# Weights of the feature-major products: high part by a rounding DMA, low part by an accumulating DMA

## The chip, the cores and the metric

The kernel runs on one core of a Trainium2 chip. The metric is the device time of one execution in microseconds (us), lower is better; runs of the kernel before and after are compared as medians. The core has five engines that run apart and meet at semaphores: TensorE (PE, matmul; PEld is its weight load), VectorE (DVE), ScalarE (ACT), GpSimd (POOL) and SyncE (SP, which here only issues transfers). Transfers (DMA) run on 16 DMA engines, whoever issues them.

## What is computed

One encoder layer, in float32, for two requests that share all weights: `p` with 512 positions and `s` with 1024, both 1024 wide.

```python
h = rms_norm(x, g_pre_mix) * (1.0 + sc1) + sh1          # sh, sc, gt: from silu(c) @ w_ada
u = h @ w_in                                            # split into xa, ya, xb, ga, gb
xa = depthwise_conv(xa, conv_w, conv_b, CONV_A_LEFT)
h_fwd, h_bwd = rg_lru(xa, ...), rg_lru(xa, ..., reverse=True)
y_a = ((h_fwd + h_bwd) * jax.nn.gelu(ya)) @ w_a_out
y_b = fourier_mix(xb) @ w_b_out
merged = jax.nn.sigmoid(ga) * y_a + jax.nn.sigmoid(gb) * y_b
x = x + gt1 * rms_norm(merged @ w_o, g_post_mix)
h = rms_norm(x, g_pre_ffn) * (1.0 + sc2) + sh2
up = depthwise_conv(h @ w_up, ffn_conv_w, ffn_conv_b, CONV_F_LEFT)
f = (jax.nn.gelu(gate) * val) @ w_down                  # val, gate: the halves of up
x = x + gt2 * rms_norm(f, g_post_ffn)
```

## The kernel before

**Products.** Every large product runs in three passes on fp32r operands: weight and activation are each split into a high part (the value rounded to fp32r) and a low part (the rest, rounded), and high x high, high x low and low x high are added up in PSUM. In the feature-major products (w_xa, w_ya, w_ga, w_gb, w_a, and w_up for `p` and for three groups of `s`) the weight stands as the stationary operand. `fm_mm` loops over the 8 slices of 128 input rows and in each over the passes in the order of `passes`: weight high with activation high, weight high with activation low, weight low with activation high. So the third matmul of a unit is the first that reads the low part of its weight (in `s`, where each pass has two halves of 512 columns, the fifth).

**Units and steps.** The work is one list of steps. A step may have a `Unit`, a weight tile of 128 x 1024 (512 KB), which is 24 matmuls of 512 columns in `p` and 48 in `s`. In `p` two units fill one PSUM tile, and what follows on ACT and DVE (`post`) comes after the second. `emit` walks the list: before the matmuls of step i it calls `prep_to`, which prepares the units up to three ahead (`AHEAD`), and `load_to`, which issues loads up to three units (`RAW_BUFS`) beyond the prepared ones. The order in which `emit` issues is the order on each engine; nothing is reordered after.

**One unit's weights.** `load_unit` (L124) has SP load the tile into `raw` (3 buffers). `prep_unit` takes an `hl` tile (4 buffers, high and low part) and calls `split`: ACT copies `raw` into the high part (L109; units that are not `on_act` use DVE, L111) and DVE subtracts the high part from `raw` into the low part (L112).

**What stands around them on the queues.** In the first stage of `p`, the recurrent units (`lru_step`) follow each other: after their matmuls ACT runs 8 tanh (L684), 4 exponentials (L692), 4 tanh (L694) and two Relu (L696), later two square roots (L710). The gate products end in a tanh on ACT (L737), the `ya` products in a Gelu on ACT (L776), a product on DVE (L777) and a split (`yh`, `yl`). In the merge stage (`merge_steps`) pairs of w_a units alternate with pairs of w_b units (13 matmuls of 258 columns each), and the RMSNorm of the other request's rows is woven in: ACT squares a row tile with a sum (L413), POOL makes the reciprocal root in two one-column operations (L430, L431), ACT scales (L418). In the up stage of `p` (`up_steps`) 22 pairs of units follow each other; after each pair ACT runs the centre tap (L1339, twice) and DVE the outer taps (L1347), and after every other pair, the gate half, ACT runs the Gelu (L1361). Lines are those of the profile; in the changed file the code below the edits stands 19 lines further down (L696 there is L715, L1361 is L1380).

Of the kernel before, what the change touches and what calls it, by code (L numbers as in the profile page):

```python
# [10 lines left out]
F32 = mybir.dt.float32  # L11
F32R = mybir.dt.float32r
AF = mybir.ActivationFunctionType
ALU = mybir.AluOpType
# [4 lines left out]
KT = D // 128  # L19
# [9 lines left out]

BIG_BUFS = 40  # L30
RAW_BUFS = 3
HL_BUFS = 4
AHEAD = 3
PAIR_AHEAD = 3
# [17 lines left out]
class Seq:  # L52
    def __init__(self, name, idx, n, x, y):
        self.name, self.idx, self.n, self.x, self.y = name, idx, n, x, y
        self.nf = 1024 // n
        self.tt = n // 128
        self.chunks = n // 512
        self.groups = KT // self.nf
        self.pq_tiles = self.tt // 2


class Unit:
    def __init__(self, src, cols, mix=False, on_act=False, whole=True):
        self.src, self.cols, self.mix, self.on_act, self.whole = src, cols, mix, on_act, whole
        self.raw = self.hi = self.lo = None

# [6 lines left out]
class Enc:  # L73
# [46 lines left out]
            nc.vector.tensor_tensor(out=out[:, 1, :], in0=src, in1=out[:, 0, :].bitcast(F32), op=ALU.subtract)  # L120

    def load_unit(self, u):
        u.raw = self.sb.tile([128, u.cols], F32, tag="raw", bufs=RAW_BUFS, name=self.nm("raw"))
        self.nc.sync.dma_start(out=u.raw, in_=u.src)  # L124

    def prep_unit(self, u):
        hl = self.sb.tile([128, 2, u.cols], F32R, tag="hl", bufs=HL_BUFS, name=self.nm("hl"))
        u.hi, u.lo = hl[:, 0, :], hl[:, 1, :]
        src = u.raw
        if u.mix:  # L130
            nc = self.nc
            src = self.big([128, u.cols], name="wb")
            ab = u.raw[:, 0:512].rearrange("p (s c) -> p s c", s=2)
            nc.vector.tensor_tensor(out=src[:, 0:256], in0=ab[:, 0, :], in1=ab[:, 1, :], op=ALU.add)
            nc.vector.tensor_tensor(out=src[:, 256:512], in0=ab[:, 1, :], in1=ab[:, 0, :], op=ALU.subtract)
            nc.vector.tensor_copy(src[:, 512:640], u.raw[:, 512:640])
        if u.mix:
            self.split(u.hi, u.lo[:, 0:512], src, keep=512)
            nc.vector.tensor_tensor(
                out=u.hi[64:96, 512:640], in0=src[64:96, 512:640], in1=u.hi[64:96, 512:640].bitcast(F32), op=ALU.subtract)  # L140
            return
        self.split(u.hi, u.lo, src, act=u.on_act)
# [9 lines left out]

    def load_to(self, k):
        while self.ld < min(len(self.units), k):
            if self.units[self.ld].unit is not None:
                self.load_unit(self.units[self.ld].unit)
            self.ld += 1

    def prep_to(self, k):
        while self.pp < min(len(self.units), k):  # L160
            self.load_to(self.pp + 1)
            u = self.units[self.pp]
            if u.pre is not None:
                u.pre()
            if u.unit is not None and u.unit.whole:
                self.prep_unit(u.unit)
            self.pp += 1
            self.load_to(self.pp + RAW_BUFS)

    def emit(self):  # L170
        pos = 0
        for i, s in enumerate(self.steps):
            while self.rl < min(len(self.steps), i + LOAD_AHEAD + 1):
                for f in self.steps[self.rl].loads:
                    f()
                self.rl += 1
            self.load_to(self.pp + RAW_BUFS)
            self.prep_to(pos + AHEAD + 1)
# [54 lines left out]
    def fm_steps(self, sq, table, tiles, xh, xl, post, on_act=False):  # L233
        box = {}
        steps = []
        for f, m in enumerate(tiles):
            u = Unit(table[m], KT * 128, on_act=on_act)

            def mm(u=u, f=f):
                if f == 0:  # L240
                    box["ps"] = self.ps([128, sq.nf, sq.n])
                self.fm_mm(self.fm_chunks(sq, box["ps"], f), u, 0, xh(), xl())

            steps.append(Step(mm=mm, unit=u))
        steps[-1].post = lambda: post(box.pop("ps"))
        return steps
# [927 lines left out]
    def up_quads(self, sq, hb, dst, plain):  # L1174
# [64 lines left out]
        for g in range(plain, FT):  # L1239
# [3 lines left out]
            def part(i, src, w=w):  # L1243
                if ring["n"] % 2 == 0:
                    ring["t"] = self.sb.tile([128, 2, 1024], F32R, tag="hl", bufs=HL_BUFS, name=self.nm("wq"))
                h = ring["n"] % 2
# [323 lines left out]
```

## Time and profile before

| | us |
|---|---|
| median of 3 runs | 2103.56 |
| their range | 2102.67 to 2103.68 |
| the profiled execution | 2103.23 |
| its span, first to last instruction | 2101.1 |

| engine | busy us | share of the span |
|---|---|---|
| PE | 2068.3 | 98% |
| DVE | 1420.8 | 68% |
| ACT | 944.8 | 45% |
| POOL | 55.3 | 3% |

The profiled execution lies within the range of the timed ones, and 2.1 us of it lie around the span. PE is busy nearly throughout at a granted clock of 0.997, so PE's idle time is the only time that can be taken away without making matmuls fewer or faster; it lies in the first 350 us and at the very end. The trace has about one DMA engine in three busy on the mean (135 GB/s).

### The profile page before, as it was taken

What the parts mean: (1) busy time and instruction counts of PE and PEld (TensorE: products, weight loads), DVE (VectorE), ACT (ScalarE), POOL (GpSimd) and SP (SyncE); (2) the same over time, 40 slices, a digit from 0 to 9 for tenths busy, and PEclk for the clock granted to TensorE, in tenths of its full rate; (3) what the DMA queues carried; (4) which work ended last, traced back from release to release, by engine and by line L of the source; (5) the groups of instructions that cost most, each with busy time, mean ns of one, the idle gap of its engine ahead of it and who ended that gap; (6) DMA issues with size and microseconds to landing.
All of it is one profiled execution on the core that took longest, in us unless ns stands there. A gap on an engine that the chain in (4) does not pass through costs nothing.

```text
span 2101.1 us, 24339 instructions
## 1 busy us (share of the span) xinstructions
PE 2068.3 (98%) x9602; PEld 1687.5 (80%) x9602; DVE 1420.8 (68%) x1798; ACT 944.8 (45%) x1213; POOL 55.3 (3%) x132
## 2 busy tenths in 40 slices
PE   7999999999999999999999999999999999999998
PEld 6777778888888888888888888888888888888887
DVE  4677888677667664656576445749687887875553
ACT  2377555355565632135333336633344444454442
POOL 0000010000000000000100001000000000000000
PEclk9999999999999999999999999999999999999999
DMA  9643475632233314343543324332122222284422
GB/s 342 206 131 130 145 259 188 236 135 96 100 105 99 112 50 145 121 146 122 217 147 116 111 96 166 100 123 88 61 76 83 83 81 81 100 313 165 143 92 109
DMA packets 91121, 284.57 MB, mean 135 GB/s; under 512 B 9056, under 2 KB 20736, under 8 KB 91008
## 3 DMA queue, kind: packets, MB, share of 16 engines
q1 hardware_dynamic: 91008, 283.03, 39.3%
q8 instruction: 75, 1.23, 0.2%
q14 instruction: 38, 0.31, 0.0%
HBM read 237.87 MB, written 45.12 MB: 135 GB/s over the span
## 4 chain that ended last, share of the span: by engine, by line
PE 87%; DVE 5%; ACT 4%; issue 2%; DMA 2%; POOL 0%; SPq 0%; DVEq 0%; POOLq 0%; ACTq 0%
PE ps L201 86%; PE ps L204 1%; DVE hl L112 1%; ACT th L684 1%; ACT th L694 1%; DVE xc L658 1%; ACT ea L692 1%; DMA hr<-hrowp 1%; ACT xn L413 0%; DVE th L715 0%; DVE th L720 0%; DVE th L718 0%; DMA x<-in_x_sample_dram 0%; DMA x<-in_x_prompt_dram 0%; ACT hl L109 0%
## 5 line engine op out<-in xcount | busy, mean ns | idle before, releaser
L201 PE MATMUL ps<-hh,hl 128*128 128x512 f32 x2144 | 632.6, 394 | 3.5 <-DVE hl L112 3.0
L201 PEld LDWEIGHTS ps<-hh,hl 128*128 128x128 f32 x2144 | 402.2, 188 | 99.5 <-DVE hl L112 4.3
L201 PE MATMUL ps<-hl,ah 128*128 128x512 f32 x1440 | 452.3, 395 | 0.0
L112 DVE TENSOR_TENSOR hl<-raw,hl 128x1024 fp32r<-128x1024 f32 (+2 forms) x240 | 286.8, 1200 | 172.3 <-ACT hl L109 170.8
L201 PE MATMUL ps<-hl,hl 128*128 128x512 f32 x1072 | 380.8, 394 | 0.0
L201 PE MATMUL ps<-hx,wq 128*128 128x512 f32 x1596 | 370.9, 394 | 0.0
L109 ACT ACTIVATE hl<-raw 128x1024 fp32r<-128x1024 f32 (+1 forms) x222 | 232.5, 1053 | 279.3 <-PE ps L201 235.2
L201 PEld LDWEIGHTS ps<-hx,wq 128*128 128x128 f32 x1596 | 299.7, 188 | 71.0 <-DVE wq L1251 0.2
L201 PEld LDWEIGHTS ps<-hl,ah 128*128 128x128 f32 x1440 | 269.0, 188 | 61.8
L201 PE MATMUL ps<-hl,al 128*128 128x512 f32 x720 | 283.9, 394 | 0.0
L201 PEld LDWEIGHTS ps<-hl,hl 128*128 128x128 f32 x1072 | 201.4, 188 | 47.6
L201 PEld LDWEIGHTS ps<-hl,al 128*128 128x128 f32 x720 | 135.2, 188 | 32.0
L1347 DVE SCALAR_TENSOR_TENSOR cf<-ps,vec,cf 128x511 f32<-128x511 f32 (+1 forms) x100 | 75.3, 808 | 83.7 <-ACT cf L1339 83.5
L201 PE MATMUL ps<-yh,hl 128*128 128x512 f32 x384 | 111.8, 394 | 0.6 <-DVE yb L991 0.3
L1250 ACT ACTIVATE wq<-wsum 128x512 fp32r<-128x512 f32 x76 | 46.1, 629 | 118.0 <-DVE wsum L1261 118.0
L1195 DVE SCALAR_TENSOR_TENSOR cf<-cq,vec,cf 128x1023 f32<-128x1023 f32 x76 | 97.1, 1277 | 0.0
L1339 ACT ACTIVATE cf<-ps,vec 128x512 f32<-128x512 f32 (+1 forms) x50 | 39.1, 827 | 105.8 <-PE ps L201 105.8
L201 PEld LDWEIGHTS ps<-yh,hl 128*128 128x128 f32 x384 | 71.5, 188 | 17.6 <-DVE yb L991 0.8
L112 DVE TENSOR_TENSOR al<-fq,ah 128x512 fp32r<-128x512 f32 x88 | 57.2, 686 | 32.3 <-PE ps L201 18.4
L201 PE MATMUL ps<-hx,hl 128*128 128x512 f32 x288 | 66.9, 394 | 0.0
L201 PE MATMUL ps<-yl,hl 128*128 128x512 f32 x192 | 65.3, 394 | 0.0
L658 DVE SCALAR_TENSOR_TENSOR xc<-ps,vec,xc 128x511 f32<-128x511 f32 (+3 forms) x48 | 46.9, 1012 | 25.7 <-ACT xc L650 25.1
(182 smaller groups left out, 2325.0 us busy)
## 6 DMA issues: line engine op xcount, KB each, us to landing
raw<-in_w_up_dram SPq DMA_DIRECT2D x88, 512.0 KB, 3.5
raw<-in_w_down_dram SPq DMA_DIRECT2D x66, 512.0 KB, 3.5
ada<-in_w_adaT_dram SPq DMA_DIRECT2D x32, 512.0 KB, 4.9
raw<-in_w_o_dram SPq DMA_DIRECT2D x24, 512.0 KB, 3.5
fs<-cf SPq DMA_DIRECT2D x22, 512.0 KB, 2.6
fq<-fs SPq DMA_DIRECT2D x22, 512.0 KB, 6.0
ada<-in_w_ada_dram SPq DMA_DIRECT2D x16, 512.0 KB, 8.5
raw<-in_w_gb_dram SPq DMA_DIRECT2D x16, 512.0 KB, 4.3
```

Of the source, the lines that this page charges most:

```text
L109: nc.scalar.activation(out=hi, in_=src, func=AF.Copy)
L112: nc.vector.tensor_tensor(out=lo, in0=src[:, 0:keep], in1=hi[:, 0:keep].bitcast(F32), op=ALU.subtract)
L201: self.nc.tensor.matmul(*args, **kw)
L204: self.nc.tensor.transpose(*args)
L658: nc.vector.scalar_tensor_tensor(out=xc[:, f, o], in0=ps[:, f, o.start + d:o.stop + d], scalar=w[:, tap:tap + 1], in1=xc[:, f, o], op0=ALU ...
L684: nc.scalar.activation(out=t[:, f, :], in_=ps[:, f, :], func=AF.Tanh, scale=0.5, bias=self.halfb[:, b:b + 1])
L692: nc.scalar.activation(out=ea[:, f, :], in_=r[:, f, :], func=AF.Exp, scale=self.nk4[:, k:k + 1], bias=self.nk4[:, k:k + 1])
L694: nc.scalar.activation(out=r[:, f, :], in_=r[:, f, :], func=AF.Tanh, scale=self.k2[:, k:k + 1], bias=self.k2[:, k:k + 1])
L1195: nc.vector.scalar_tensor_tensor(out=box[key][:, o], in0=c[:, i], scalar=self.vec[:, V_FW + 3 * m + t:V_FW + 3 * m + t + 1], in1=box[key][ ...
L1250: nc.scalar.activation(out=hi, in_=src, func=AF.Copy)
L1339: nc.scalar.activation(out=acc[:, f, :], in_=ps[:, f, :], func=AF.Identity, scale=w[:, 1:2], bias=self.vec[:, V_FB + m:V_FB + m + 1])
L1347: nc.vector.scalar_tensor_tensor(out=acc[:, f, o], in0=ps[:, f, o.start + d:o.stop + d], scalar=w[:, tap:tap + 1], in1=acc[:, f, o], op0=A ...
```

## The change

The units of the feature-major products (118 in all: 34 in the mixing and merge stages of `p`, 32 in the heads and `ya` of `s` and 8 in its merge, 44 in the up stage of `p`) no longer use `raw` or DVE. Their `hl` tile is taken at the load. POOL issues a DMA that reads the weight and writes it rounded to fp32r into the high part (L128 of the changed file); ACT writes the negated high part into the low part (L135, the same size as the copy that it replaces); then POOL issues a second DMA that reads the weight again and adds it onto the low part (L136). `load_to` holds such a unit back until it is at most one beyond the next to be prepared, and `prep_to` prepares it one step later than other units, after it has issued the next unit's load.

```diff
+DMA_LO = True
     def load_unit(self, u):
+        if u.dma:
+            hl = self.sb.tile([128, 2, u.cols], F32R, tag="hl", bufs=HL_BUFS, name=self.nm("hl"))
+            u.hi, u.lo = hl[:, 0, :], hl[:, 1, :]
+            self.nc.gpsimd.dma_start(out=u.hi, in_=u.src)
+            return
...
     def prep_unit(self, u):
+        if u.dma:
+            self.nc.scalar.activation(out=u.lo, in_=u.hi.bitcast(F32), func=AF.Copy, scale=-1.0)
+            self.nc.gpsimd.dma_start(out=u.lo, in_=u.src, accum_op=ALU.add)
+            return
...
     def load_to(self, k):
         while self.ld < min(len(self.units), k):
+            u = self.units[self.ld].unit
+            if u is not None and u.dma and self.ld > self.pp + 1:
+                return
...
     def prep_to(self, k):
         while self.pp < min(len(self.units), k):
             self.load_to(self.pp + 1)
             u = self.units[self.pp]
+            if u.unit is not None and u.unit.dma and self.pp + 2 > k:
+                break
+            if u.unit is not None and u.unit.dma:
+                self.load_to(self.pp + 2)
...
-            u = Unit(table[m], KT * 128, on_act=on_act)
+            u = Unit(table[m], KT * 128, on_act=on_act, dma=DMA_LO)
```

ACT in the first recurrent step of `p`, kernel before: the end of the recurrent unit's chain (the names `th`), and the copy `hl_1214`, which belongs to the fourth unit that PE runs after the recurrent one.

```order
L694 ACTIVATE th_1179<-th_1179,k_104 128x512
L696 ACTIVATE th_1179<-th_1179 128x1024
L109 ACTIVATE hl_1214<-raw_1075 128x1024
L710 ACT_TABLE_LOAD
L710 ACTIVATE th_1159<-th_1159 128x1024
L710 ACTIVATE th_1179<-th_1179 128x1024
L650 ACTIVATE xc_1282<-ps_1219,vec 128x512 x2
```

The same place of the changed kernel; `hl_1098` belongs to the third unit after the recurrent one, `hl_1143` to the fourth.

```order
L713 ACTIVATE th_1168<-th_1168,k_104 128x512
L715 ACTIVATE th_1168<-th_1168 128x1024
L135 ACTIVATE hl_1098<-hl_1098 128x1024
L729 ACT_TABLE_LOAD
L729 ACTIVATE th_1148<-th_1148 128x1024
L729 ACTIVATE th_1168<-th_1168 128x1024
L135 ACTIVATE hl_1143<-hl_1143 128x1024
```

The third unit's ACT instruction moved from a place ahead of the whole chain to the place behind its last Relu, and the fourth's from there to behind the square roots. The other three recurrent steps of `p` show the same.

ACT in the up stage of `p`, kernel before: centre taps and Gelu of one pair (`cf_8434`, from `ps_8377`), then the copies for the fourth and the fifth unit that PE runs after that pair.

```order
L1339 ACTIVATE cf_8434<-ps_8377,vec 128x512 x2
L1361 ACTIVATE cf_8434<-cf_8434 128x1024
L109 ACTIVATE hl_8442<-raw_8333 128x1024
L109 ACTIVATE hl_8474<-raw_8373 128x1024
L1339 ACTIVATE cf_8504<-ps_8449,vec 128x512 x2
```

The changed kernel, a Gelu of the same kind; `hl_8415` and `hl_8446` belong to the third and the fourth unit after the pair `ps_8419`.

```order
L1358 ACTIVATE cf_8473<-ps_8419,vec 128x512 x2
L1380 ACTIVATE cf_8473<-cf_8473 128x1024
L135 ACTIVATE hl_8415<-hl_8415 128x1024
L135 ACTIVATE hl_8446<-hl_8446 128x1024
L1358 ACTIVATE cf_8542<-ps_8489,vec 128x512 x2
```

Each copy stands one unit later on ACT against PE's work than it did.

POOL in the merge stage of `p`, kernel before: only the two operations of each RMSNorm.

```order
L430 TENSOR_SCALAR sm_2384<-sm_2380 128x1
L431 TENSOR_TENSOR sm_2381<-sm_2384,mhalf 128x1
L430 TENSOR_SCALAR sm_2414<-sm_2410 128x1
L431 TENSOR_TENSOR sm_2411<-sm_2414,mhalf 128x1
L430 TENSOR_SCALAR sm_2449<-sm_2445 128x1
L431 TENSOR_TENSOR sm_2446<-sm_2449,mhalf 128x1
```

The changed kernel at the first w_a pair behind w_b units (`hl_2291`, `hl_2340`): DMA rows stand among them.

```order
L128 DMA hl_2340<-in_w_a_dram 128x1024
L449 TENSOR_SCALAR sm_2356<-sm_2352 128x1
L450 TENSOR_TENSOR sm_2353<-sm_2356,mhalf 128x1
L449 TENSOR_SCALAR sm_2381<-sm_2377 128x1
L450 TENSOR_TENSOR sm_2378<-sm_2381,mhalf 128x1
L136 DMA hl_2291<-in_w_a_dram 128x1024
L449 TENSOR_SCALAR sm_2415<-sm_2411 128x1
L450 TENSOR_TENSOR sm_2412<-sm_2415,mhalf 128x1
L136 DMA hl_2340<-in_w_a_dram 128x1024
```

The RMSNorm operations now queue behind the loads of high parts, each of which waits for PE to be done with the unit that held its buffer.

## Rows read from the trace of the kernel before

**Rows 1.** The page, busy us (share of the span) and instructions by engine.
```profile
PE 2068.3 (98%) x9602; PEld 1687.5 (80%) x9602; DVE 1420.8 (68%) x1798; ACT 944.8 (45%) x1213; POOL 55.3 (3%) x132
```

**Rows 2.** Busy time by stretch: from:to, length, busy us of each engine, PEclk, DMA share, GB/s.
```profile
100.00:150.00 50.00, 43.67 (x218) 34.84 (x217) 36.73 (x41) 32.96 (x42) 0.00 (x0) 1.00 0.40 129
150.00:200.00 50.00, 48.82 (x212) 39.25 (x211) 37.25 (x36) 39.48 (x49) 0.00 (x0) 1.00 0.47 158
200.00:250.00 50.00, 47.15 (x201) 37.20 (x200) 40.17 (x41) 34.38 (x40) 0.00 (x0) 1.00 0.36 127
250.00:300.00 50.00, 46.75 (x231) 38.52 (x230) 45.63 (x79) 21.35 (x30) 5.81 (x8) 0.97 0.67 230
...
1100.00:1200.00 100.00, 100.00 (x433) 80.84 (x432) 61.90 (x81) 35.17 (x41) 0.00 (x0) 1.00 0.33 111
```

**Rows 3.** Waits of PE over the span: waited for, us in total, times, longest.
```profile
PE ps L201 <- DVE hl L112: 4.9, 8, 1.9
```

**Rows 4.** The page's costliest groups: busy us, mean ns of one | idle before, releaser.
```profile
L112 DVE TENSOR_TENSOR hl<-raw,hl 128x1024 fp32r<-128x1024 f32 (+2 forms) x240 | 286.8, 1200 | 172.3 <-ACT hl L109 170.8
```

**Rows 5.** DMA issues: out<-in, queue, count, size, median us from issue to landing.
```profile
raw<-in_w_up_dram SPq DMA_DIRECT2D x88, 512.0 KB, 3.5
...
ada<-in_w_ada_dram SPq DMA_DIRECT2D x16, 512.0 KB, 8.5
```

**Rows 6.** Timeline, first recurrent step of p: start us, us, engine, line, operation.
```profile
116.47 4.72 ACT L684 ACTIVATE th<-ps,halfb 128x512 f32<-128x512 f32 x8
...
128.53 1.06 ACT L696 ACTIVATE th<-th 128x1024 f32<-128x1024 f32 x1
129.50 1.04 ACT L109 ACTIVATE hl<-raw 128x1024 fp32r<-128x1024 f32 x1
129.95 0.63 PE L201 MATMUL ps<-hh,hl 128*128 128x512 f32 x2
```

**Rows 7.** Timeline, the same two rows in the third and the fourth recurrent step.
```profile
200.29 1.04 ACT L109 ACTIVATE hl<-raw 128x1024 fp32r<-128x1024 f32 x1
...
202.05 0.63 PE L201 MATMUL ps<-hh,hl 128*128 128x512 f32 x2
...
231.51 0.62 PE L201 MATMUL ps<-hh,hl 128*128 128x512 f32 x2
231.55 1.04 ACT L109 ACTIVATE hl<-raw 128x1024 fp32r<-128x1024 f32 x1
```

**Rows 8.** Timeline, up stage of p: the copies behind one Gelu, and a later matmul.
```profile
1120.99 1.99 ACT L109 ACTIVATE hl<-raw 128x1024 fp32r<-128x1024 f32 x2
...
1127.12 0.63 PE L201 MATMUL ps<-hh,hl 128*128 128x512 f32 x2
```

**Rows 9.** Timeline, merge stage of p: last Gelu of ya and PE's matmuls.
```profile
266.88 1.03 ACT L776 ACTIVATE gl<-ps 128x1024 f32<-128x1024 f32 x1 [1.95 <-PE ps L201]
...
271.82 0.39 PE L201 MATMUL ps<-yh,hl 128*128 128x512 f32 x1
...
285.20 0.65 PE L201 MATMUL ps<-z,hl 128*128 128x258 f32 x4
...
295.65 0.62 PE L201 MATMUL ps<-yh,hl 128*128 128x512 f32 x2
...
306.34 0.52 PE L201 MATMUL ps<-z,hl 128*128 128x258 f32 x3
...
309.93 0.39 PE L201 MATMUL ps<-yh,hl 128*128 128x512 f32 x1
```

**Rows 10.** Timeline, merge stage of p: the RMSNorm on POOL and ACT.
```profile
311.36 0.51 POOL L430 TENSOR_SCALAR sm<-sm 128x1 f32<-128x1 f32 x1 [5.33 <-ACT xn L413]
311.95 0.55 POOL L431 TENSOR_TENSOR sm<-sm,mhalf 128x1 f32<-128x1 f32 x1
312.53 1.15 ACT L418 ACTIVATE xn<-x,sm 128x1024 f32<-128x1024 f32 x1 [1.26 <-POOL sm L431]
...
314.54 1.05 ACT L413 ACTIVATE xn<-x 128x1024 f32<-128x1024 f32 x1
```

More of the change, by code (lines that the diff above doesn't have):

```diff
@@ L62, with __init__ @@
 class Unit:
-    def __init__(self, src, cols, mix=False, on_act=False, whole=True):
+    def __init__(self, src, cols, mix=False, on_act=False, whole=True, dma=False):
+        self.dma = dma
         self.src, self.cols, self.mix, self.on_act, self.whole = src, cols, mix, on_act, whole
```

## The prediction

> **What bounds the kernel now.** First the page's engine line: PE is busy for 2068.3 of 2101.1 us [rows 1]. A stretch in which PE never idles holds 433 matmuls in 100 us, 0.231 us each [rows 2], so a unit is 24 x 0.231 = 5.56 us of PE in `p` and 11.1 us in `s`. Only idle time of PE can be won, and the busy times by stretch say where it is: 6.33 + 1.18 + 2.85 + 3.25 = 13.6 us between 100 and 300 us, the four stretches in which PE falls short of 50 [rows 2], and none in the up stage of `p`. Then the waits of PE: the largest part that has a name in those stretches is the DVE subtract, 4.9 us in 8 waits [rows 3]. So DVE work matters in the first 300 us and nowhere else, though 118 of the 240 subtracts (1200 ns each, 142 us) go [rows 4].
>
> **What the change removes.** 118 subtracts on DVE: 84 of them (40 in `s`, 44 in the up stage) lie beside a PE that never waits for them and are worth nothing. The 34 in the first stages of `p` take 34 x 1.2 = 41 us of load off DVE where it holds PE up. I credit all the idle time of 100 to 300 us, less the 3.25 us of the last stretch, which stay in the reckoning of the merge stage below: **-10.4 us**. The removed loads on SP (3.5 us to landing [rows 5]) were hidden three units ahead: nothing. ACT's negated copy is of the size of the one it replaces: nothing by itself.
>
> **What it adds: a landing behind ACT's copy.** Before, 1.2 us of DVE lay between ACT's copy and a usable low part. Now a transfer lies there, L us from the copy's end to landing. No row shows an accumulating DMA, nor one that POOL issues. Below: 3.5 us, the same 512 KB read once by SP [rows 5]. Above: 8.5 us, the slowest group of 512 KB, when all DMA engines are busy [rows 5]. I take L = 6, nearer to the middle than to either row: 3.5, plus 1.1 for a turn of POOL (its nearest row, the pair of one-column operations from 311.36 to 312.50 [rows 10]), plus 1.5 for reading as many bytes again: at a DMA share of 0.33 the trace moves 111 GB/s, 336 at full share [rows 2], and 524 KB at 336 GB/s take 1.56 us. The Trainium skill ("DMA: Bandwidth & Descriptors", Anatomy of one DMA) fits a transfer issued by GpSimd as 2.0 us plus bytes at 436 GB/s, an estimate of 3.2 us here and about that of our lower row; the total by it would be 2120.
>
> **What it moves.** The order rows show that ACT's copy stands one unit later against PE's work than before. Where that puts it behind a chain that starts at PE's last pair, a lead that was comfortable is used up. The low part is needed by a unit's third matmul.
>
> *Heads of `p`, four recurrent steps.* The third unit behind the recurrent one is now copied where the fourth was: behind the last Relu. That place ends at 129.50 + 1.04 = 130.54, and the third unit's third matmul started at 129.95 [rows 6]: 0.6 us too late before the transfer has begun. ACT's chain there is its own (tanh from 116.47 on [rows 6]), so less DVE work doesn't shorten it. In the third step the place ends 0.7 us before the matmul, in the fourth 1.1 us behind it [rows 7]; the second is like the first. Mean 0.4 too late: 4 x (L + 0.4) = **+25.6 us**. The fourth unit's low part comes behind the square roots, some 4 us later, and PE reaches it 5.56 us later: covered.
>
> *Up stage of `p`, 22 pairs.* Behind the Gelu of every second pair stand two copies, 1120.99 to 1122.98, the first done at about 1122.0 [rows 8]. In the changed order it serves the unit whose third matmul ran at 1127.12 [rows 8]: lead 5.1 us. The second has 5.56 - 0.95 us more and is covered, as are the copies behind the pairs without a Gelu. 11 x (L - 5.1) = **+9.9 us**. The high part is loaded once PE has left a buffer, three units or 16.7 us ahead, and its landing plus the copy fit into that: nothing.
>
> *Merge stage of `p`, four pairs of w_a units.* First pair: the copy is now behind the last `ya` split, a chain that starts with the Gelu at 266.88: 1.03, the product on DVE and the split's copy 1.2 + 1.05, this copy 1.05, done at 271.2; the third matmul was at 271.82 [rows 9]. L - 0.6 = +5.4. Third pair: POOL's RMSNorm operations now queue behind a high part's load, which waits for PE to finish the second w_a unit before it; ACT's scaling waits for POOL, and the copy stands behind two such rounds on ACT. From PE's last matmul of that unit (just before 306.5 [rows 9]): one issue on POOL, at a price of 1, then 1.1, scaling 1.15, squares 1.05 + 0.2, 1.1, 1.15 [rows 10], copy 1.05: 7.8 us, plus L. PE's third matmul of the third pair starts at 309.93 [rows 9], only 3.4 us after the same point. L + 4.4 = +10.4. Second pair: the same 7.8 + L from 285.85 (end of the w_b unit's matmuls that start at 285.20), against 295.65 [rows 9], 9.8 us with the stalls of before in them: +4.0. Fourth pair: no RMSNorm stands ahead, only one POOL issue: 1 + L - 3.6 = +3.4. Together **+23.2 us**.
>
> *Queues passed.* On POOL only the RMSNorm operations are overtaken; in the row stages their results wait for no one on PE. SP loses 118 loads and its other loads come no later. In `s` a unit lasts 11.1 us, so a copy one unit later still leaves one whole unit, 11 us, for L: nothing.
>
> **Sum.** -10.4 + 25.6 + 9.9 + 23.2 = +48 us on the profiled 2103.2 (span 2101.1 and 2.1 around it; the median is 0.3 above): **2151.5**. At L = 3.5: heads 15.6, up 0, merge 2.9 + 1.5 + 7.9 + 0.9 = 13.2, sum +18, so 2122. At L = 8.5: 35.6, 37.4, 33.2, sum +96, so 2199.
>
> **Rivals.**
>
> *The transfers do not keep up* (slower still). In the up stage a unit's plain load is 0.524 MB in 5.56 us, 94 GB/s or a share of 0.28; the rest of the 0.33 [rows 2] is 0.05. If the rounding and the accumulating DMA take c plain loads of DMA time together, the share is 0.05 + 0.28 c, over 1 from c = 3.4. At c = 5 (rounding twice a plain load, adding three times) it is 1.45: 44 x 5.56 x 0.45 = 110 us, and between 100 and 300 us, where the mean share is 0.475, of which 34 x 1.56 / 200 = 0.265 are the 34 loads, 0.21 + 5 x 0.265 = 1.53: 200 x 0.53 = 106 us. With little of the short leads beside it, about 2320; from c = 4 on it is over 2200. For it: nothing bounds c from above in this trace. Against it: only the second read is certain, c = 3, a share of 0.89. The Trainium skill ("Collectives: The Full Stack", The bandwidth ceiling) says that an add inside the DMA costs two source reads and no cycles of its own; no run here shows it, and by it the add alone would not saturate.
>
> *Faster.* DVE's relief counts in full and the low parts land in time, at 2103.2 - 10.4 = 2093. It is decided in the recurrent steps and the merge stage: the sum of the terms above passes zero at L of about 0.8 us, under any landing in the trace. So it needs the copies to run earlier than ACT's order and chain say, by five us or so at each of the four recurrent steps; DVE's relief could do that only if it shortened ACT's chain, which waits for PE and itself.
>
> *No change* needs the same with a part of the landing left: 2099 to 2107.
>
> **How the numbers follow.** About 0.2%, 4 us, is what a measurement of this kernel can tell from no change. Short leads with L between 3.5 and 8.5, taken 10 us wider below since DVE's relief may also pull some copies forward, and 15 wider above for longer landings when DMA is crowded: 2112 to 2215, chance 0.74. Transfers that do not keep up: 0.16, 2200 to 2340. Faster 0.06, no change 0.04. The range reaches from 2112 to 2260: it leaves out 0.10 below and about 0.10 of the saturated cases above. Faster 0.06, same 0.04, slower 0.90; the predicted time is that of the likeliest case.
>
> **What would show each step.** 122 subtracts left on L112 and 118 fewer rows on DVE. PE waiting for a DMA onto `hl` four times between 110 and 260 us by some 6 us each, four times in the merge stage by 3 to 10, and at every fourth unit of the up stage by about 1; no such wait in `s`. The median time from issue to landing of the accumulating DMA gives L, and with it each term. PE's waits for DVE in the first 300 us gone. A DMA share near 1 and waits at every unit of the up stage would show the first rival; a landing behind the copy that PE doesn't wait for in the recurrent steps would show that the order was read wrongly.

## The result, and the profile after

The changed kernel takes 2185.09 us (median of 4 runs, 2184.3 to 2185.7) against 2103.37 us before: a ratio of 1.0389, 95% interval 1.0371 to 1.0407. It is 81.7 us slower; 48 were forecast, and the time lies inside the range of 2112 to 2260 that was given. The profiled execution spans 2182.9 us against 2101.1, which is 81.8 more.

The page of the changed kernel: busy time by engine; the DMA queues (packets, MB, share of 16 engines; SP's loads are q1, POOL's are q0); the subtracts that are left; the landing times.

```profile
PE 2092.9 (96%) x9602; PEld 1702.7 (78%) x9602; DVE 1287.4 (59%) x1680; ACT 946.2 (43%) x1213; POOL 223.0 (10%) x368
...
q1 hardware_dynamic: 74016, 221.16, 28.7%
q0 software_dynamic: 33984, 123.75, 25.2%
...
L114 DVE TENSOR_TENSOR hl<-raw,hl 128x1024 fp32r<-128x1024 f32 (+3 forms) x122 | 144.0, 1180 | 108.6 <-ACT hl L111 107.7
...
hl<-in_w_up_dram POOLq DMA_DIRECT2D x88, 512.0 KB, 6.9
...
raw<-in_w_up_dram SPq DMA_DIRECT2D x44, 512.0 KB, 3.4
```

Two readings answer to [rows 1]. PE's idle time went from 2101.1 - 2068.3 = 32.8 us to 2182.9 - 2092.9 = 90.0 us, 57.2 more. And PE's *busy* time grew by 24.6 us with the same 9602 matmuls. Together they are the 81.8 us, and the second part stands nowhere in the prediction's sum. DVE lost 133 us of work, as meant, and POOL gained 168 us of issuing.

The waits of PE over the span, to be set beside [rows 3]: what was waited for, us in total, times, longest.

```profile
PE ps L220 <- DMA hl<-in_w_a_dram: 27.8, 5, 10.7
PE ps L220 <- DMA hl<-in_w_up_dram: 16.1, 12, 5.3
PE ps L220 <- DMA hl<-in_w_gb_dram: 13.1, 3, 5.5
...
PE ps L220 <- DMA hl<-in_w_ya_dram: 6.7, 2, 5.2
PE ps L220 <- DMA hl<-in_w_xa_dram: 4.9, 1, 4.9
...
PE ps L220 <- DVE hl L114: 0.4, 2, 0.2
```

The waits for the split weights are 27.8 + 16.1 + 13.1 + 6.7 + 4.9 = 68.6 us in 23 places. The idle time that is left, 90.0 - 68.6 = 21.4, is 11.4 less than before. Most of that is DVE's relief: the wait for the subtract fell from 4.9 to 0.4. Some of it may be that PE, held up at the new waits, finds other work done.

Where the 24.6 us of busy time come from is seen in the stretches (from:to, length, PE busy, granted clock, DMA share, GB/s):

```profile
100.00:150.00 50.00, 45.06 (x241) 0.93 0.65 163
...
300.00:350.00 50.00, 37.77 (x175) 0.80 0.75 229
350.00:400.00 50.00, 37.07 (x161) 0.80 0.55 155
```

Before, PE's clock was 1.00 in nearly all of this part [rows 2]. Closer, around one wait of the merge stage (the same columns, 2 us each), and the start of PE's rows behind that wait (start, duration, engine, line, operation):

```profile
328.00:330.00 2.00, 0.00 (x0) 0.50 0.92 176
...
336.00:338.00 2.00, 2.00 (x9) 0.83 0.08 27
338.00:340.00 2.00, 2.00 (x10) 1.00 0.00 0
```

```profile
331.17 1.22 PE L220 MATMUL ps<-yh,hl 128*128 128x512 f32 x2 [5.99 <-DMA hl<-in_w_a_dram]
332.19 0.63 PE L220 MATMUL ps<-yl,hl 128*128 128x512 f32 x1
332.62 1.05 PE L220 MATMUL ps<-yh,hl 128*128 128x512 f32 x2
```

In this wait the granted clock is 0.50, the lower of its two levels (1.2 of 2.4 GHz); it had fallen between 322 and 324 us, at two shorter waits of PE. When the low part lands, matmuls start 0.43 us apart (332.19, 332.62) instead of 0.23, for some 5 us; then the clock is back. PE's rows show the same behind each of the eight long waits of `p`'s first stages, behind the long one of the up stage, and behind two shorter ones (2.7 and 1.9 us): six to thirteen matmuls 0.43 us apart, 1.3 to 2.5 us lost at each. Taken together, PE is busy for 55.4 us at 0.50 in the changed kernel and for 6.8 before. At full clock the same work takes half of that, so 24.3 of the 24.6 us are the clock.

Before, no wait between 30 and 350 us was longer than 1.9 us, but one of that length was followed by such a stretch, in the merge stage (PE's rows before; twelve matmuls of 258 columns take 1.62 us ahead of the wait and six take 1.49 behind it):

```profile
283.37 1.62 PE L201 MATMUL ps<-z,hl 128*128 128x258 f32 x12
...
289.76 0.98 PE L201 MATMUL ps<-z,hl 128*128 128x258 f32 x6 [1.86 <-DVE mg L1000]
...
293.06 1.49 PE L201 MATMUL ps<-z,hl 128*128 128x258 f32 x6
```

The granted clock is 0.50 from 291.2 to 294.6 us there, which is the 0.97 of the stretch from 250 to 300 in [rows 2]. The same holds at the start of that trace, from 28.3 to 31.8 us, where matmuls of 512 columns start 0.43 us apart. Behind the other wait of 1.86 us before, which ends at 244.61, nothing is slow. So a wait of just under 2 us can go either way, and each of the changed kernel's nine longest waits for a low part (3.96 to 10.73 us) is followed by a slow stretch.

The Trainium skill has this ("TensorE: Matmul & The Clock Gate", HAM oscillation): a wait for a DMA between tiles sends PE back to half clock, and the cost is paid at every such wait. The trace agrees for those nine waits, and the prediction had left it out.

### The profile page after: what moved, and what is told of

It is laid out like the page before. It is cut to its first block, busy times and chain, and to the rows that moved or that the text cites. A ratio compares the mean times of both kernels' runs of the same rounds, so it can differ in the third digit from the quotient of the medians.

```text
span 2182.9 us, 24512 instructions
## 1 busy us (share of the span) xinstructions
PE 2092.9 (96%) x9602; PEld 1702.7 (78%) x9602; DVE 1287.4 (59%) x1680; ACT 946.2 (43%) x1213; POOL 223.0 (10%) x368
## 3 DMA queue, kind: packets, MB, share of 16 engines
q1 hardware_dynamic: 74016, 221.16, 28.7%
q0 software_dynamic: 33984, 123.75, 25.2%
## 4 chain that ended last, share of the span: by engine, by line
PE 83%; DMA 7%; issue 6%; ACT 2%; POOL 1%; DVE 0%; SPq 0%; POOLq 0%; DVEq 0%; ACTq 0%
PE ps L220 82%; DMA hl<-in_w_up_dram 3%; DMA hl<-in_w_a_dram 1%; PE ps L223 1%; DMA hl<-in_w_ya_dram 1%; DMA hl<-in_w_gb_dram 1%; POOL hl L128 0%; ACT th L713 0%; DMA wxbt<-in_wxbT_dram 0%; ACT hl L135 0%; ACT ea L711 0%; DMA hl<-in_w_xa_dram 0%; ACT xn L432 0%; POOL sm L450 0%; POOL sm L1112 0%
## 5 line engine op out<-in xcount | busy, mean ns | idle before, releaser
L220 PE MATMUL ps<-hh,hl 128*128 128x512 f32 x2144 | 645.5, 401 | 40.9 <-DMA hl<-in_w_up_dram 16.1
L220 PEld LDWEIGHTS ps<-hh,hl 128*128 128x128 f32 x2144 | 408.2, 191 | 145.5 <-DMA hl<-in_w_up_dram 21.4
L220 PE MATMUL ps<-hl,hl 128*128 128x512 f32 x1072 | 386.0, 399 | 0.0
L114 DVE TENSOR_TENSOR hl<-raw,hl 128x1024 fp32r<-128x1024 f32 (+3 forms) x122 | 144.0, 1180 | 108.6 <-ACT hl L111 107.7
L135 ACT ACTIVATE hl<-hl 128x1024 fp32r<-128x1024 f32 x118 | 123.1, 1051 | 135.6 <-DMA hl<-in_w_up_dram 70.7
L111 ACT ACTIVATE hl<-raw 128x1024 fp32r<-128x1024 f32 (+1 forms) x104 | 109.7, 1055 | 166.3 <-PE ps L220 144.8
L220 PE MATMUL ps<-yh,hl 128*128 128x512 f32 x384 | 119.3, 415 | 28.9 <-DMA hl<-in_w_a_dram 27.8
L220 PEld LDWEIGHTS ps<-yh,hl 128*128 128x128 f32 x384 | 75.9, 200 | 48.5 <-DMA hl<-in_w_a_dram 30.2
L1101 POOL TENSOR_SCALAR sm<-sm 128x1 f32<-128x1 f32 x48 | 10.8, 229 | 820.4 <-ACT junk L1099 819.6
L114 DVE TENSOR_TENSOR al<-fq,ah 128x512 fp32r<-128x512 f32 x88 | 57.3, 687 | 32.9 <-PE ps L220 18.4
L722 DVE SCALAR_TENSOR_TENSOR th<-th,xc 128x1024 f32<-128x1024 f32 x24 | 29.3, 1225 | 71.0 <-ACT th L703 69.5
```

What stands on the lines that cost most here:

```text
L111: nc.scalar.activation(out=hi, in_=src, func=AF.Copy)
L114: nc.vector.tensor_tensor(out=lo, in0=src[:, 0:keep], in1=hi[:, 0:keep].bitcast(F32), op=ALU.subtract)
L135: self.nc.scalar.activation(out=u.lo, in_=u.hi.bitcast(F32), func=AF.Copy, scale=-1.0)
L220: self.nc.tensor.matmul(*args, **kw)
L722: nc.vector.scalar_tensor_tensor(out=i, in0=i, scalar=1.0, in1=xc, op0=ALU.add, op1=ALU.mult)
L1101: nc.gpsimd.tensor_scalar(out=sums[o][:, half:half + 1], in0=sums[o][:, half:half + 1], scalar1=1.0 / D, scalar2=sums[o][:, 0:1] if half e ...
```

## The waits, seen one by one

First recurrent step of `p`, changed kernel (timeline, columns as above; in brackets the idle time before and what ended it): the copy of the third unit, its accumulating DMA, and PE's third matmul of that unit.

```profile
129.09 1.04 ACT L135 ACTIVATE hl<-hl 128x1024 fp32r<-128x1024 f32 x1
...
130.57 0.87 POOL L136 DMA_DIRECT2D hl<-in_w_gb_dram  x1 [10.12 <-ACT hl L135]
...
136.01 1.22 PE L220 MATMUL ps<-hh,hl 128*128 128x512 f32 x2 [4.94 <-DMA hl<-in_w_gb_dram]
```

The copy ends at 130.13 and PE starts at 136.01: L = 5.9 us, where 6 was taken. The copy ends 0.9 us before PE first needs the low part (136.01 - 4.94 = 131.07), where the prediction had it 0.6 us behind in this step, so the wait is 4.94 and not 6.6.

Third pair of the merge stage: POOL's load of a high part behind PE, the RMSNorm on POOL and ACT, the copy, the DMA, PE.

```profile
345.03 0.61 POOL L128 DMA_DIRECT2D hl<-in_w_a_dram  x1 [12.56 <-PE ps L220]
...
347.59 1.15 ACT L437 ACTIVATE xn<-x,sm 128x1024 f32<-128x1024 f32 x1 [12.90 <-POOL sm L450]
...
351.77 1.04 ACT L135 ACTIVATE hl<-hl 128x1024 fp32r<-128x1024 f32 x1
...
358.98 1.22 PE L220 MATMUL ps<-yh,hl 128*128 128x512 f32 x2 [10.73 <-DMA hl<-in_w_a_dram]
```

The RMSNorm of another request's rows stands still on POOL behind a load that waits for PE, ACT waits 12.9 us for it, and the copy behind it ends at 352.81: 7.8 us behind the load's issue, the 7.8 of the prediction. From there to PE's matmul are 6.2, and PE waits 10.7 (10.4 were forecast).

Up stage, the longest wait:

```profile
1236.30 0.87 POOL L136 DMA_DIRECT2D hl<-in_w_up_dram  x1 [5.87 <-ACT hl L135]
...
1236.87 0.86 POOL L128 DMA_DIRECT2D hl<-in_w_up_dram  x1
...
1237.44 1.19 POOL L136 DMA_DIRECT2D hl<-in_w_up_dram  x1
...
1246.51 1.22 PE L220 MATMUL ps<-hh,hl 128*128 128x512 f32 x2 [5.26 <-DMA hl<-in_w_up_dram]
```

Three weight transfers are issued within 1.2 us on POOL (and five loads on SP from 1235.96 to 1238.06), and the first of them lands 10.2 us after its issue; at most of the other Gelus the first low part lands after 5.1 to 6.4. The other eleven waits of this stage are 16.1 - 5.3 = 10.8 us. Eight of them stand at units whose copy is the first behind a Gelu, as forecast, and come to 6.9 us. Three, 3.9 us, stand at other units at the start of the stage (PE's matmuls at 1110.11, 1131.00 and 1138.30), where low parts landed 7.8 to 13 us after their issue and the DMA share was 0.97 (1110 to 1160 us); no term had these.

## The experiments

The theory at the start: a low part that is copied one unit later and then lands 5.9 us after the copy comes too late at the places that the prediction names, and each long wait costs a stretch at half clock besides. The rivals: the rate of the DMA engines; the position alone, whatever makes the low part; the adding DMA as such; stages that act on each other. Where a run is compared with the kernel before, that is the one that ran on the same chip beside it (2103.1 to 2104.5 us); a comparison with the changed kernel is across chips, and good to 1 or 2 us.

**Filling the waits (e1).** PE repeats a harmless first matmul while it would wait.

```diff
+WARM = {6: 20, 10: 20, 16: 22, 20: 21, 26: 21, 28: 24, 30: 44, 32: 16}
...
+        if u.dma:
+            for _ in range(WARM.get(self.seen, 0)):
+                for out, cols in outs:
+                    self.mmul(out, lhsT=u.hi[:, 0:128], rhs=xh[0][:, cols], start=True, stop=True)
+            self.seen += 1
```

> The changed kernel with one thing added: ahead of eight units (the four units of the recurrent steps and the four w_a units at which PE waited 4 to 11 us for a low part) PE runs the unit's first matmul 16 to 44 times more, so that it is busy for most of the wait and nothing starts earlier. Theory (a long wait costs twice: the wait, and then 9 to 13 matmuls at a granted clock of 0.5, 0.43 us each instead of 0.23): the waits stay as long but are filled, the eight slow stretches go, 8 x 2.3 = 18 us less, 2167 us. Rival (the slow matmuls come from the transfers that run beside them, or from the unit's place in the program): they stay, 2185 us or a little above. Second rival (filling the wait makes it longer): above 2186.

Measured: 2171.9 us, 13.2 less than the changed kernel, by doing 188 matmuls more. The page's engine line and the same stretches as above:

```profile
PE 2120.0 (98%) x9790; PEld 1725.8 (80%) x9790; DVE 1287.2 (59%) x1680; ACT 945.9 (44%) x1213; POOL 222.4 (10%) x368
```

```profile
100.00:150.00 50.00, 49.72 (x274) 1.00 0.70 173
...
300.00:350.00 50.00, 46.63 (x230) 0.97 0.81 267
350.00:400.00 50.00, 49.28 (x241) 1.00 0.54 148
```

The granted clock is 1.00 where it was 0.93 and 0.80, at about the same DMA share or a higher one, so the transfers are not what slowed the matmuls. 188 x 0.231 = 43.4 us of PE's busy time are the repeats; the rest is 2120.0 - 43.4 = 2076.6, 16.3 us less than in the changed kernel. Only 13.2 of them reach the time, since idle time and repeats together are 50.0 + 43.4 = 93.4 us against 90.0 idle before: the waits became 3.4 us longer in all. The 18 us of the expectation were a little high because a slow stretch costs nearer 2.0 us than 2.3. Five waits of 2 to 5 us stay unfilled, and behind three of them the clock still falls. The clock part of the loss is shown.

**The low part last (e2).**

```diff
-        for k in range(nk):
-            for q, (w, x) in enumerate(self.passes(u, xh, xl)):
+        for k, q in sorted(((k, q) for k in range(nk) for q in range(3)), key=lambda t: u.dma and t[1] == 2):
+            w, x = self.passes(u, xh, xl)[q]
```

> The changed kernel with the three passes of a feature-major unit in another order: the sixteen matmuls that read the high part first, then the eight that read the low part, so the low part is needed at the seventeenth matmul instead of the third, 14 x 0.231 = 3.2 us later in p. Theory (short leads before the low part): every wait shrinks by 3.2 us. Recurrent steps and ya 23 to 7 us of waits, merge 26 to 13, up 16 to 2, and the slow stretches go wherever the wait falls under 2 us, which leaves one or two of ten (22 of 24.5 us go): 2185 - 43 - 22 = 2120 us. Rival (the DMA engines do not keep up, so that the waits are a matter of rate): a later need delays nothing in the long run, the waits come back at later units, above 2165 us.

Measured: 2136.2 us (2134.4 and 2138.0), 49 us less than the changed kernel with the same transfers; 65 were expected. The waits for `w_up` fall from 16.1 to 4.5 us, those for `w_a` from 27.8 to 13.7. A rate limit would not yield to this, so lead time is the matter. Of the shortfall some 9 us are waits for low parts, 31.1 us where 22 were expected, most of them in the recurrent steps and `ya` (12.9 for 7) and in the up stage (4.5 for 2). Some 7 us are slow stretches: PE's busy time fell by 15.3 us and not by 22. The merge stage came out as expected in sum, but not evenly:

```profile
PE ps L220 <- DMA hl<-in_w_a_dram: 13.7, 4, 9.7
```

The longest wait there, at the third pair, is still 9.7 us. A PE that comes sooner to it finds the same chain of POOL and ACT, which is argued from the rows and not tested.

**The order alone (e3).** The kernel before, its splits issued one unit later.

```diff
             u = self.units[self.pp]
+            if u.unit is not None and u.unit.late and self.pp + 2 > k:
+                break
...
-            u = Unit(table[m], KT * 128, on_act=on_act)
+            u = Unit(table[m], KT * 128, on_act=on_act, late=True)
```

> The kernel before with only the move: feature-major units are prepared one unit later, as in the change, but still loaded by SP and split by ACT and DVE. Theory (the late copy costs because a landing of 5.9 us stands behind it): with 1.2 us of DVE in its place the four recurrent steps cost 4 x (0.4 + 1.4) = 7 us, the up stage nothing since its lead is 5 us, the merge stage 1 or 2, and no wait is long enough to bring the clock down: 2110 to 2114 us. Rival (the position alone is the cost, through ACT's and DVE's queues): above 2130. No change at all would say that leads are not used up by the position.

Measured: 2133.9 us, 29 us slower than the kernel before (ratio 1.0141, 1.0112 to 1.0171). The theory, at 7 to 10 us, fell here, and so did its word that no wait would bring the clock down: PE's idle time grew by 18.1 us and its busy time by 11.9 (2080.2 of 2131.1 us). A wait of PE, and what stands ahead of it on ACT and DVE:

```profile
PE ps L204 <- DVE hl L113: 26.8, 14, 4.9
```

```profile
132.08 1.04 ACT L110 ACTIVATE hl<-raw 128x1024 fp32r<-128x1024 f32 x1
...
138.38 1.23 DVE L726 TENSOR_TENSOR th<-th,th 128x1024 f32<-128x1024 f32 x1
139.52 1.22 DVE L113 TENSOR_TENSOR hl<-raw,hl 128x1024 fp32r<-128x1024 f32 x1
...
140.80 1.22 PE L204 MATMUL ps<-hh,hl 128*128 128x512 f32 x2 [4.80 <-DVE hl L113]
```

It is another unit that waits: the fourth, whose copy now stands behind the square roots. The copy is done at 133.1, but the subtract queues on DVE behind the scans and products of the recurrent step until 139.52. In the changed kernel the same copy is followed by a DMA, which does not queue on DVE, and PE doesn't wait there. So the late position is costly with either means of making the low part, but by different waits: with DVE at the fourth unit, through DVE's queue; with the DMA at the third, through the landing. The 29 us are not a part of the 82 that could be taken off them.

**A plain second DMA (e4).**

```diff
-            self.nc.gpsimd.dma_start(out=u.lo, in_=u.src, accum_op=ALU.add)
+            self.nc.gpsimd.dma_start(out=u.lo, in_=u.src)
```

> The changed kernel with the second DMA as a plain rounding write instead of an accumulating one, so the low part holds the rounded weight (the product is another, the work and the order are the same). Theory (the landing of 5.9 us is that of a transfer issued by POOL, rounding or adding alike: in the trace the rounding ones take 6.2 us from issue to landing and the accumulating ones 6.4): landing 6 to 6.4 us, time 2175 to 2186. Rival (adding is what costs): landing near the 3.5 us of SP's plain loads, waits of 2.4 us less at each site, most slow stretches gone, about 2125 us.

Measured: 2149.4 us in the one run, 36 less than the changed kernel. Neither side of the expectation held: the landing falls, but not to SP's.

```profile
PE 2084.0 (97%) x9602; PEld 1699.5 (79%) x9602; DVE 1287.1 (60%) x1680; ACT 944.3 (44%) x1213; POOL 179.6 (8%) x368
...
q0 software_dynamic: 33984, 123.75, 18.4%
...
hl<-in_w_up_dram POOLq DMA_DIRECT2D x88, 512.0 KB, 4.5
```

The 236 rounding loads use 18.4% of 2147.6 us on the 16 DMA engines, 1.67 us each. With 118 of them accumulating it was 25.2% of 2182.9, 550 us; less 118 x 1.67 that is 353, or 2.99 us for an accumulating one, if the rounding ones beside it still take 1.67. SP's queue uses 28.7% of 2182.9 us for 221.16 MB of all its transfers, on the mean 1.48 us for 0.524 MB. So an accumulating transfer costs 2.0 plain ones of DMA time, and both together c = 3.1. The Trainium skill ("Collectives: The Full Stack", The bandwidth ceiling) counts two source reads and no extra cycles for an add. The 2.0 fits it; that the second read is what takes the time, no run shows.

The landing follows: the median is 4.5 us for a load issued by POOL when nothing adds, and 6.2 (rounding) and 6.4 (accumulating) when half of them add. Whether the others land later because they share POOL's queue or because they share the 16 DMA engines is not told apart. Of L some 1.9 us are the add; 1.0 is POOL's issue against SP's. Of the 35.3 us by which the span is shorter, 26.4 are idle time of PE (63.6 against 90.0) and 8.9 are busy time. The forecast's terms give nearly that idle time for 1.9 us of landing, 4 x 1.9 + 11 x 0.9 + 4 x 1.9 = 25.1, and have nothing for the busy time.

**One stage at a time (e5, e6, e12).** In each run only the named units carry the change.

```diff
-            u = Unit(table[m], KT * 128, on_act=on_act, dma=DMA_LO)
+            u = Unit(table[m], KT * 128, on_act=on_act, dma=DMA_LO and table is self.a["w_up"] and sq.name == "p")
```

> The change in the up stage of p alone (44 of the 118 units); the rest as before. Theory (the cost is the sum of local waits and the slow clock behind the long ones): what that stage gave in the changed kernel, 16 us of waits and 7 us of slow matmuls, 2103 + 23 = 2126 us, and PE's waits at every second pair. Forecast of the step as written: 10 us, 2113. Rival (the stages act on each other, by the queue of POOL or by the buffers): off by over 5 us from 2126.

> The change in the units of s alone (40 of 118); the rest as before. Theory: a unit lasts 11.1 us there, so one later leaves room for a landing; only one wait of 2.0 us stood there in the changed kernel: 2103 to 2106 us. Rival (twice the weight traffic and POOL's queue cost everywhere): 2110 or above. Rival on the other side (less DVE work helps in s): 2101 or below.

> The change in the first stages of p alone (34 of 118: recurrent heads, ya, merge). Theory (the stages add up): the whole change is 81.7 us, the up stage alone gave 21.4 and s alone 3.6, so 56.7 are left: 2160 us, 2157 to 2163. Rival (the stages act on each other, so that the parts do not add up): off by over 5 us from it.

Measured against the kernel before beside each: the up stage 2124.5 us, +21.4; `s` 2106.7, +3.6 (ratio 1.0015, 1.0004 to 1.0025); the first stages of `p` 2157.0, +53.8. The sum is 78.8 of 81.7 us, so the parts add up to within 3. That is a little luckier than it looks: in the trace of the up stage's run, stretches at half clock stand also at 110 to 114 and 247 to 250 us, behind waits of 1.6 and 1.9 us in parts that this run doesn't change, and cost some 3 of the 21.4 us. The up stage has 11.4 us of waits for `hl` here instead of 16.1, with a longest of 3.7 instead of 5.3; why is not shown. In `s` 1.8 us are one wait for `w_a`; less DVE work helps nothing there.

**The most that can be won (e7).**

```diff
+        if u.nosub:
+            self.nc.scalar.activation(out=u.hi, in_=src, func=AF.Copy)
+            u.lo = u.hi
+            return
```

> The kernel before without the subtract of the feature-major units on DVE: the third pass reads the high part again (so the product lacks its low x high part), and nothing takes the subtract's place. It prices what the change can give at most. Theory: the waits of PE for DVE between 100 and 300 us, 13.6 us of idle time, of which I credited 10.4: 2092 to 2096 us. Rival (DVE's other work or ACT's chain ends last there anyway): 2099 or above.

Measured: 2089.3 us, ratio 0.9936 (0.9921 to 0.9951): 13.9 us faster, with PE busy for 2063.9 of 2087.1 us. Idle time fell by 9.6 us and busy time by 4.4; the slow stretch at 291 us is gone with them. That prices the subtract's removal with nothing in its place; this kernel leaves out the product of the low weight with the high activation. With the other steps as they stand, a change that takes the subtract away can win 14 us, and this one put 68.6 us of waits there.

**The copy a unit earlier (e8, e9, e10).** A fifth buffer lets the copy stand where it stood before the change. In e8 the next high part is issued behind this unit's low part (`more` is 0 throughout), in e9, whose edit stands here, ahead of it; e10 is e9 with the low part last. Room for the buffer comes from three small tags.

```diff
-HL_BUFS = 4
+HL_BUFS = 5
...
-            if u is not None and u.dma and self.ld > self.pp + 1:
+            if u is not None and u.dma and self.ld > self.pp + more:
...
-            if u.unit is not None and u.unit.dma and self.pp + 2 > k:
-                break
             if u.unit is not None and u.unit.dma:
-                self.load_to(self.pp + 2)
+                self.load_to(self.pp + 2, 1)
```

> The changed kernel with a fifth buffer for the split weights (room made in three small tags), so that ACT's copy stands one unit earlier, where it stood before the change; all else as in the change. Theory (the lead that was used up is one unit, 5.6 us in p): waits in the recurrent steps fall from 5 us to 0 or 1, those of the merge stage by 5 us each (about 6 us are left, most at the third pair), the up stage has none, one slow stretch is left: 2095 to 2106 us. Rival (rate of the DMA engines, share 0.83 in the up stage): above 2140. Rival (POOL's queue: a high part's load that waits for PE holds up the low part's transfer behind it whatever the order): above 2120.

Measured: 2346.6 us, far on the other side. The up stage of e8, ACT and POOL:

```profile
1200.80 0.86 POOL L136 DMA_DIRECT2D hl<-in_w_up_dram  x1 [12.82 <-ACT hl L135]
1201.36 0.88 POOL L128 DMA_DIRECT2D hl<-in_w_up_dram  x1
...
1207.84 1.06 ACT L135 ACTIVATE hl<-hl 128x1024 fp32r<-128x1024 f32 x1 [6.13 <-DMA hl<-in_w_up_dram]
...
1209.33 0.86 POOL L136 DMA_DIRECT2D hl<-in_w_up_dram  x1 [7.10 <-ACT hl L135]
```

From one low part's issue to the next are 8.5 us: the high part's issue, its landing, the copy. PE needs a new unit every 5.56 us, so this chain sets the pace. It was the edit's order on POOL that made it, not the earlier copy, as e9 shows.

> As e8_early (five buffers, ACT's copy one unit earlier, where it stood before the change), but the next unit's high part is issued on POOL ahead of this unit's low part, as in the change. In e8_early it stood behind it, and the units became a chain: low part issued, next high part issued, some 6 us of landing, copy 1.05 us, next low part issued, 8.4 us a unit where PE needs 5.56. Theory (position): the waits of 5 us in the recurrent steps and ya go, in the merge stage 5 us of the third pair and one slow stretch (2.4) are left, the up stage waits under 5 us in all, and DVE's relief is what the kernel without the subtract gained, 14 us: 2103 - 14 + 5 + 2 + 3 = 2099, range 2092 to 2108. Rival (the transfers' rate, or ACT's queue standing still for the high part, 6.2 us of landing against 5.56 us of PE a unit): waits in the up stage at most units, above 2120.

> e9_five and the pass order of e2_lo_last together: the copy a unit earlier, and the low part needed 3.2 us later. Theory: what waits are left in e9_five shrink by 3.2 us each; at most one of 2 us stays (third pair of the merge stage): 2089 to 2096 us, faster than the kernel before by 7 to 14 us. Rival (waits of ACT for high parts set the pace): as far above as e9_five, less a few us.

Measured: e9 2130.4 us, e10 2123.1 us, ratios 1.0127 (1.0110 to 1.0144) and 1.0092 (1.0077 to 1.0107). The earlier copy, with the fifth buffer that it needs, takes back 55 of the 82 us, so most of the loss is the position. But 2092 to 2108 had been expected of e9 and 2089 to 2096 of e10. What is left in e9, at the first recurrent step:

```profile
109.66 0.90 POOL L136 DMA_DIRECT2D hl<-in_w_xa_dram  x1 [5.49 <-ACT hl L135]
...
110.30 0.83 POOL L128 DMA_DIRECT2D hl<-in_w_gb_dram  x1
...
117.73 1.06 ACT L135 ACTIVATE hl<-hl 128x1024 fp32r<-128x1024 f32 x1 [5.83 <-DMA hl<-in_w_gb_dram]
118.69 2.98 ACT L701 ACTIVATE th<-ps,halfb 128x512 f32<-128x512 f32 x5
...
120.00 0.79 PE L218 MATMUL ps<-hh,hl 128*128 128x512 f32 x1 [3.98 <-ACT th L701]
```

A high part's load stood on POOL behind a low part that waited for ACT; it landed 7.4 us later; ACT stood still for it, and with ACT the tanh that would have freed PSUM for PE. Between 60 and 400 us ACT's copies wait 73 us for high parts in e9 and 43 in the changed kernel. An earlier copy moves part of the wait from the low part's landing to the high part's. That this accounts for all 27 us that e9 still loses is argued from these rows; no run takes it away alone.

**The pass order in the kernel before (e11).** The edit of e2 without the change.

> The kernel before, nothing of the change, with only the pass order of e2_lo_last: in the feature-major units the low part of the weight is needed at the seventeenth matmul instead of the third (3.2 us later in p). Theory: the 4.9 us in which PE waits for the subtract go, and what small extra time of matmuls stands behind them: 2096 to 2100 us. Rival (another wait, for ACT's high part or for DVE's other products, ends there instead): 2101 to 2104.

Measured: 2101.9 against 2103.2 us, ratio 0.9993 (0.9984 to 1.0002): no change that can be told. The waits for the subtract (L113 here) go from 4.9 to 1.7 us, but those for DVE's rounding copy of weights that it splits alone (L112 here) from 2.0 to 3.5, and one for ACT's high part comes. So other waits end there instead, as the rival had it:

```profile
PE ps L202 <- DVE hl L112: 3.5, 3, 1.7
...
PE ps L202 <- DVE hl L113: 1.7, 5, 0.5
...
PE ps L202 <- ACT hl L110: 1.0, 1, 1.0
```

So no version here that computes the whole product beats the kernel before.

## Why the prediction was right, and where it was short

*What bounds it, and DVE's relief.* Credited with 10.4 us, measured 11.4 as idle time that went; without any substitute it was 9.6 of idle time and 13.9 in all (e7). The 84 subtracts beside a busy PE were worth nothing, as said: from 400 to 1350 us PE is busy throughout before and in e7.

*The landing.* L was taken as 6, between 3.5 and 8.5; it is 5.9 to 6.6 in the four recurrent steps and 6.2 in the third merge pair. Its make-up was right in size: 1.1 for POOL (measured 1.0), 1.5 for the second read (the add brings 1.9, with whatever it does to the transfers beside it). The estimate of 3.2 us that the prediction worked out from the Trainium skill ("DMA: Bandwidth & Descriptors", Anatomy of one DMA) lies under the 4.5 us that a rounding load issued by POOL takes in e4.

*Recurrent steps and `ya`.* 25.6 us forecast; the four waits are 4.94, 4.88, 5.48 and 5.22, 20.5 in all, since the copies ended 0.9 to 1.3 us ahead of PE's need, where the trace of before had put them 0.4 behind it on the mean. A first `gb` unit (2.7 us) and a `ya` unit (1.5) waited too, which were not foreseen: 24.7.

*Merge stage.* 5.4, 4.0, 10.4 and 3.4 us forecast; 5.1, 6.0, 10.7 and 4.0 measured, 25.8 against 23.2. The coupling through POOL's queue was the right mechanism, as the rows of the third pair show.

*Up stage.* 9.9 us forecast, 16.1 measured: 12.2 at nine units behind a Gelu, of which 5.3 at one where transfers crowd, and 3.9 at three units at the stage's start that no term had. `s`: nothing forecast, 2.0.

*The rate of the DMA engines.* Not the bound of the stage. At c = 3 the prediction had a share of 0.89; c is 3.1, and between 1110 and 1320 us the measured share is 0.85. In the first 50 us of that it is 0.97, and the three unforeseen waits stand there.

*The step that failed* is the frame of the sum itself: every wait was put in at its own length, and every matmul behind it at 0.231 us, the price of a stretch in which PE never idles [rows 2]. Waits on low parts are 68.6 us where the three terms had 58.7; with the relief that would have given some 57 us against 48. The other 24.6 us of the 81.8 are matmuls at half clock behind the long waits, shown by the granted clock and by e1. At about 2 us behind each of eight waits of the forecast, 16 us could have been put in beforehand. The trace of before had the price, in the stretch at 0.50 behind a wait of 1.86 us in the merge stage, which [rows 2] shows as 0.97. The section of the Trainium skill that states the rule ("TensorE: Matmul & The Clock Gate", HAM oscillation) was not weighed either. The range held because it was wide: it reached up for longer landings and for the rival of the rate, not for the clock, so that part of its holding is luck. The measured loss is 1.7 times the forecast one.

## What to carry to other kernels

When PE is the bound, a new wait of some microseconds costs its length and then, here, about 2 us more for a stretch of matmuls at half clock. Repeated matmuls in the wait got most of that part back. Before a step on an engine is replaced by a transfer, put its landing (here 6 us instead of 1.2) against the lead at every place where the step stands behind a long chain, not against the mean lead, and look at what else waits in the issuing engine's queue: on POOL a load that waited for PE held up an RMSNorm, and through it ACT. Price the best case first: removing the subtract with nothing in its place won 14 us, which is the size of what any substitute for it could have won here.

## What the runs showed of the hardware that was not expected

- An accumulating DMA of 512 KB took 2.99 us of the 16 DMA engines, a rounding one 1.67, SP's transfers 1.48 on the mean for as many bytes. Beside accumulating ones the rounding loads' median landing was 6.2 us instead of 4.5.
- A clock that fell to 0.50 at a wait of PE stayed there for six to thirteen matmuls of 512 columns after it. With PE busy for 29.5 of 30 us (1320 to 1350 us of the changed kernel) it was 1.00 at a DMA share of 0.86.
